# Linear attention on one core: K and V in four-head 4 KB runs as Q already was, the output moved between a group's first matmuls and its Q features, one PSUM pool

## The chip, the cores and the metric

One core of a Trainium2 chip. The metric is the device time of one execution in microseconds (us), the median of several. The "span" in a profile is the time from the first to the last instruction and is some 1.7 us shorter than the device time. All runs that are compared here were in the fast state (one run of the kernel before, beside experiments 6 and 10, was slow and stays out of the ratios); a kernel run once has the state unknown. In the profiles PE is TensorE (matmuls), DVE is VectorE, ACT is ScalarE, POOL is GpSimd and SP is SyncE. PSUM is the memory that TensorE writes its results to, and SBUF the one that the transfers fill. A "turn" is one pass of the main loop, over one group.

## The reference, cut to what matters

```python
# Q, K, V: (8, 12, 512, 64) float32
Q_feat = np.maximum(0, Q) + 1
K_feat = np.maximum(0, K) + 1
KV    = einsum('bhkd,bhkv->bhdv', K_feat, V)
K_sum = sum(K_feat, axis=2)
out   = (Q_feat @ KV) / (Q_feat @ K_sum + 1e-10)
```

There are 96 heads of 512 positions of 64 numbers. The kernel takes them in 12 groups of 8 heads. Inputs and output are 12.58 MB each, so 50.33 MB move whatever the kernel does.

## The kernel before: the parts that the change and the argument touch

Each group passes through four stages: features (DVE makes max(x+1, 1) of K and Q, ACT copies V beside a column of ones), KV (TensorE contracts K features with V, ACT copies the result "kva" out of PSUM), transposes (TensorE turns Q around, ACT copies "qt" out of PSUM), output (TensorE multiplies qt with kva, DVE takes reciprocals and multiplies, and a DMA stores).

```python
    # PSUM: qt_ps 2 tiles, kva_ps 1 tile, o_ps 2 tiles, each in its own pool
    # K, V: 8 positions (2 KB) per partition and head pair; Q: 16 positions (4 KB), four heads
    def kv_and_transpose(g):
        ...
        for h in range(2):
            for c in range(C):
                for j in range(2):           # 64 rows: one head on each half of the array
                    nc.tensor.matmul(kva_ps[:, j, h * W : h * W + W],
                        lhsT=kf[64 * j : 64 * j + 64, h, c, :, :],
                        rhs=va[64 * j : 64 * j + 64, h, c, 0:W], ...)
        ...                                   # 2 copies of kva on ACT
        for half in range(2):
            qt_ps = psum_qt.tile([P, C, P], BF16, name="qt_ps")     # a tile for each half
            for c in range(C):
                nc.tensor.transpose(qt_ps[:, c, :], qf[:, half * C + c, :, :], identity)
            nc.scalar.copy(out=qt[:, :, :, half], in_=qt_ps)
    ...
        for it in range(NG + 2):              # three groups in hand at once
            if it < NG:
                features(it)
            if 1 <= it < NG + 1:
                kv_and_transpose(it - 1)
            if it >= 2:
                output(it - 2)
            ...                               # load(it + 4), store(it - 3)
```

DVE, ACT and TensorE run these stages in the order in which the program gives them, as the timelines here show.

## Time and profile before

| | before |
|---|---|
| device time, median | 132.04 us |
| span | 129.8 us |
| bytes over the span | 388 GB/s |
| busiest compute engine (ACT) | 48% |
| ACT's wait for V from DMA | 48.6 us in 12 waits |

The lines for these are in the prediction below. Read "DMA" in the slices as the mean busy share of the 16 DMA engines in tenths, and a line of the timeline as start, length, engine, line, what was done, and in brackets how long the engine had been idle and what ended that.

### The profile page before, as it was taken

What the parts mean: (1) busy time and instruction counts of PE and PEld (TensorE: products, weight loads), DVE (VectorE), ACT (ScalarE), POOL (GpSimd) and SP (SyncE); (2) the same over time, 40 slices, a digit from 0 to 9 for tenths busy, and PEclk for the clock granted to TensorE, in tenths of its full rate; (3) what the DMA queues carried; (4) which work ended last, traced back from release to release, by engine and by line L of the source; (5) the groups of instructions that cost most, each with busy time, mean ns of one, the idle gap of its engine ahead of it and who ended that gap; (6) DMA issues with size and microseconds to landing.
All of it is one profiled execution on the core that took longest, in us unless ns stands there. A gap on an engine that the chain in (4) does not pass through costs nothing.

```text
span 129.8 us, 3048 instructions
## 1 busy us (share of the span) xinstructions
PE 59.0 (46%) x1344; PEld 50.5 (39%) x1344; DVE 57.7 (44%) x132; ACT 62.6 (48%) x73; POOL 36.1 (28%) x55
## 2 busy tenths in 40 slices
PE   0008309208758292864939119409606802933200
PEld 0007209107647191753828009308505701922100
DVE  0222212057374775727577077066227407567700
ACT  3023086590966939296690590391095096270000
POOL 6972224222332242224224222422231200202020
PEclk9999965555686959555595865875785685595555
DMA  2999999999999999999999999999999999999853
GB/s 93 321 204 195 210 194 204 210 206 211 205 209 208 209 207 206 210 207 207 277 302 207 253 331 205 231 350 191 218 347 223 212 357 418 420 417 360 341 218 121
DMA packets 19213, 32.17 MB, mean 248 GB/s; under 512 B 768, under 2 KB 12544, under 8 KB 19200
## 3 DMA queue, kind: packets, MB, share of 16 engines
q0 software_dynamic: 18672, 30.94, 106.3%
q1 hardware_dynamic: 528, 1.05, 2.1%
q8 instruction: 10, 0.16, 0.5%
q14 instruction: 3, 0.02, 0.0%
HBM read 37.75 MB, written 12.58 MB: 388 GB/s over the span
## 4 chain that ended last, share of the span: by engine, by line
DMA 72%; issue 19%; POOL 4%; POOLq 1%
DMA out_dram<-o_sb 31%; DMA k_raw<-in_K_dram 16%; DMA q_raw<-in_Q_dram 15%; DMA v_raw<-in_V_dram 9%; POOL out_dram L90 2%; POOLq L219 1%; POOL q_raw L86 1%; POOL k_raw L82 0%; POOL v_raw L85 0%; POOL identity masks.py:199 0%; POOL identity masks.py:197 0%; POOL v_aug L179 0%; POOLq L90 0%; POOLq L86 0%; POOLq L208 0%
## 5 line engine op out<-in xcount | busy, mean ns | idle before, releaser
L104 ACT COPY v_aug<-v_raw 128x1024 bf16<-128x1024 bf16 x24 | 24.1, 1056 | 48.6 <-DMA v_raw<-in_V_dram 48.6
L152 PE MATMUL o_ps<-kva,qt 64*64 64x65 bf16 x768 | 17.3, 229 | 46.9 <-DVE o_sb L165 45.8
L165 DVE TENSOR_TENSOR o_sb<-o_ps,recip 128x512 f32<-128x512 f32 x48 | 33.2, 691 | 1.6
L152 PEld LDWEIGHTS <-qt 64*64 64x64 bf16 x768 | 12.7, 137 | 52.0 <-DVE o_sb L165 48.9
L139 ACT COPY qt<-qt_ps 128x1024 bf16<-128x1024 bf16 x24 | 29.5, 1298 | 0.4
L118 PE MATMUL kva_ps<-v_aug,kf 64*128 64x129 bf16 x384 | 22.3, 302 | 15.4 <-ACT v_aug L104 10.1
L93 DVE TENSOR_SCALAR qf<-q_raw 128x2048 bf16<-128x2048 bf16 x12 | 8.3, 694 | 42.2 <-DMA q_raw<-in_Q_dram 42.2
L118 PEld LDWEIGHTS <-kf 64*128 64x128 bf16 x384 | 19.1, 137 | 16.2 <-issue 15.6
L138 PE MATMUL qt_ps<-identity,qf 128*128 128x128 bf16 x192 | 21.7, 303 | 0.1
L90 POOL DMA_DIRECT2D out_dram<-o_sb x12 | 9.3, 774 | 38.2 <-DVE o_sb L165 19.6
L138 PEld LDWEIGHTS <-qf 128*128 128x128 bf16 x192 | 18.8, 142 | 2.6 <-issue 2.2
L93 DVE TENSOR_SCALAR kf<-k_raw 128x1024 bf16<-128x1024 bf16 (+1 forms) x24 | 9.8, 450 | 11.2 <-DMA k_raw<-in_K_dram 11.1
L164 DVE RECIPROCAL recip<-o_ps 128x8 f32<-128x8 f32 x48 | 9.6, 201 | 10.5 <-PE o_ps L152 10.5
L85 POOL DMA_DIRECT2D v_raw<-in_V_dram x12 | 9.1, 759 | 17.0 <-ACT kva L127 5.4
L82 POOL DMA_DIRECT2D k_raw<-in_K_dram x11 | 8.6, 786 | 16.7 <-DVE kf L93 6.6
L86 POOL DMA_DIRECT2D q_raw<-in_Q_dram x12 | 8.4, 702 | 15.9 <-DMA k_raw<-in_K_dram 9.0
L127 ACT CAST kva<-kva_ps 64x260 bf16<-64x260 f32 x24 | 8.8, 367 | 3.5 <-PE kva_ps L118 3.4
L104 ACT ACT_TABLE_LOAD x1 | 1.3, 1283 | 0.7 <-PEq L208 0.7
masks.py:199 POOL TENSOR_SCALAR_AFFINE_SELECT identity<-identity 128x128 bf16<-128x128 bf16 x1 | 0.3, 287 | 0.1
masks.py:197 POOL MEMSET identity<- 128x128 bf16 x1 | 0.2, 244 | 0.0
L179 POOL MEMSET v_aug<- 128x16 bf16 x2 | 0.2, 175 | 0.0
L208 POOL MEMSET const-float32-0.0<- 128x1 f32 x1 | 0.1, 99 | 0.2 <-issue 0.2
(3 smaller groups left out, 0.3 us busy)
## 6 DMA issues: line engine op xcount, KB each, us to landing
out_dram<-o_sb POOLq DMA_DIRECT2D x12, 1024.0 KB, 20.0
v_raw<-in_V_dram POOLq DMA_DIRECT2D x12, 512.0 KB, 19.7
q_raw<-in_Q_dram POOLq DMA_DIRECT2D x12, 512.0 KB, 19.8
k_raw<-in_K_dram POOLq DMA_DIRECT2D x11, 512.0 KB, 19.7
k_raw<-in_K_dram SPq DMA_DIRECT2D x1, 1024.0 KB, 5.0
```

The lines of the kernel that those rows point to most:

```text
L85: nc.gpsimd.dma_start(out=v_raw, in_=v_dram[:, g * NP : g * NP + NP])
L86: nc.gpsimd.dma_start(out=q_raw, in_=q_dram[:, g * 2 : g * 2 + 2])
L90: nc.gpsimd.dma_start(out=o_dram[:, g * NP : g * NP + NP], in_=outs.pop(g))
L93: nc.vector.tensor_scalar(out=dst, in0=src, scalar1=1.0, scalar2=1.0, op0=ALU.add, op1=ALU.max)
L104: nc.scalar.copy(out=va[:, h].rearrange("p c (n x) -> p n c x", n=2)[:, :, :, 0:D], in_=v_raw[:, h:NP:2],)
L118: nc.tensor.matmul(kva_ps[:, j, h * W : h * W + W], lhsT=kf[64 * j : 64 * j + 64, h, c, :, :], rhs=va[64 * j : 64 * j + 64, h, c, 0:W], st ...
L127: nc.scalar.copy(out=kva[64 * n : 64 * n + 64, :, :, 0:D1], in_=kva_ps[64 * n : 64 * n + 64, :, 0 : 2 * W].rearrange("p j (h x) -> p j h x ...
L138: nc.tensor.transpose(qt_ps[:, c, :], qf[:, half * C + c, :, :], identity)
L139: nc.scalar.copy(out=qt[:, :, :, half], in_=qt_ps)
L152: nc.tensor.matmul(ops[n][64 * j : 64 * j + 64, c // 4, off : off + D1], lhsT=qt[64 * n : 64 * n + 64, c, 32 * b : 32 * b + 32, :], rhs=kv ...
L164: nc.vector.reciprocal(out=recip, in_=den)
L165: nc.vector.tensor_tensor(out=o_sb[:, 2 * n + h].rearrange("p (b r) d -> p b r d", b=2), in0=num, in1=recip.to_broadcast([P, 2, 4, D]), op ...
```

## The change

Its intent: larger contiguous runs for K and V, a store that follows closer behind the load, and a shorter way from the last landing to the last store. The core of the diff (cuts marked):

```diff
-    k_dram = view(K, C)
-    v_dram = view(V, C)
+    k_dram = view(K, C2)
+    v_dram = view(V, C2)
...
-    psum_qt = ... bufs=2;  psum_kva = ... bufs=1;  psum_out = ... bufs=2
+    psum = ctx.enter_context(tc.tile_pool(name="psum", bufs=4, ...))
...
+    def keys_values(g):                 # K features, V copies, KV, kva copies
...
+            for c in range(half * C, half * C + C):
+                for b in range(4):
+                    ps = slice(32 * b, 32 * b + 32)
+                    nc.tensor.matmul(kva_ps[b // 2][:, b % 2, 0:W],
+                        lhsT=kf[ps, c, :, :], rhs=va[ps, c, 0:W], ...)
...
+    def queries(g):                     # Q features, transposes, qt copies
+        qt_ps = psum.tile([P, 2, C, P], BF16, tag="ps", name="qt_ps")
         for half in range(2):
-            qt_ps = psum_qt.tile([P, C, P], BF16, name="qt_ps")
+            feature(qf[:, cs]..., q_raw[:, :, cs])
             for c in range(C):
-                nc.tensor.transpose(qt_ps[:, c, :], qf[:, half * C + c, :, :], identity)
-            nc.scalar.copy(out=qt[:, :, :, half], in_=qt_ps)
+                nc.tensor.transpose(qt_ps[:, half, c, :], qf[:, half * C + c, :, :], identity)
+            nc.scalar.copy(out=qt[:, :, :, half], in_=qt_ps[:, half])
...
+        for g in range(NG):
+            ...                         # load(g + 4), store(g - 2)
+            keys_values(g)
+            if g:
+                output(g - 1)
+            queries(g)
+        output(NG - 1)
```

The last group's store also goes out in two halves from SP instead of in one piece from GpSimd. Cut from the diff: each input stream gets 5 buffers instead of 4, and the Q features of a group become two instructions instead of one.

## The prediction

> **What bounds the kernel now.** I read the page from the top: first the span, the slices and the bytes, then the chain that ended last, then the waits, and last the timeline of two stretches.
>
> ```profile
> span 129.8 us, 3048 instructions
> ...
> DMA  2999999999999999999999999999999999999853
> ...
> HBM read 37.75 MB, written 12.58 MB: 388 GB/s over the span
> ...
> DMA 72%; issue 19%; POOL 4%; POOLq 1%
> ```
>
> All four compute engines are busy under half of the span (ACT is highest, at 48%), while the DMA engines stand at nine tenths or more from slice 2 to slice 37, and 72% of the chain that ended last is DMA. The kernel moves 37.75 + 12.58 = 50.33 MB. In the middle, one input tile of a group (1 MiB read as float32, cast to bf16 on the way) is issued about every 2.53 us, at the pace at which earlier ones land: 1.049 MB / 2.53 us = 415 GB/s. All bytes at that rate take 50.33 / 0.415 = 121.3 us. The other 8.5 us of the span are the start and the end: the slices fall to 8, 5 and 3 tenths there.
>
> The waits say the same. These two rows are engine, line, what was waited for, total us, times, longest:
>
> ```profile
> ACT v_aug L104 <- DMA v_raw<-in_V_dram: 48.6, 12, 6.9
> ...
> DVE qf L93 <- DMA q_raw<-in_Q_dram: 42.2, 12, 5.4
> ```
>
> Each group's copy of V waits for its data every time (12 of 12), by 4 us on average. The compute side has slack, and it has it because an iteration works on three groups at once: features of group i, both matmul stages of i-1, output of i-2. Within an iteration no stage needs what another stage made in that same iteration.
>
> The timeline gives the durations for the rest (start, us, engine, line, operation; xN = how many in a row):
>
> ```profile
> 24.18 2.01 ACT L104 COPY v_aug<-v_raw 128x1024 bf16<-128x1024 bf16 x2 [2.50 <-DMA v_raw<-in_V_dram]
> ...
> 26.86 2.45 ACT L139 COPY qt<-qt_ps 128x1024 bf16<-128x1024 bf16 x2
> ...
> 30.45 1.92 PE L118 MATMUL kva_ps<-v_aug,kf 64*128 64x129 bf16 x32
> 30.52 0.21 DVE L164 RECIPROCAL recip<-o_ps 128x8 f32<-128x8 f32 x1 [0.71 <-PE o_ps L152]
> ...
> 31.37 0.20 DVE L164 RECIPROCAL recip<-o_ps 128x8 f32<-128x8 f32 x1
> ...
> 32.21 0.75 DVE L93 TENSOR_SCALAR kf<-k_raw 128x1024 bf16<-128x1024 bf16 x2
> 32.30 1.89 PE L138 MATMUL qt_ps<-identity,qf 128*128 128x128 bf16 x16
> ...
> 34.12 0.63 PE L152 MATMUL o_ps<-kva,qt 64*64 64x65 bf16 x32
> ```
>
> To be seen: a V copy pair takes 2.01 us, a pair of transposed-Q copies 2.45; one output tile costs DVE 0.84 us (reciprocal at 30.52, the next at 31.37, the next work at 32.21); half of an output's matmuls 0.63. The last two lines that matter are at the end:
>
> ```profile
> 122.50 0.69 DVE L165 TENSOR_TENSOR o_sb<-o_ps,recip 128x512 f32<-128x512 f32 x1
> 123.49 0.75 POOL L90 DMA_DIRECT2D out_dram<-o_sb  x1 [4.21 <-DVE o_sb L165]
> ```
>
> After the last Q tile lands (107.47, where its feature starts) three groups' outputs are still to be made, one after the other, to 123.19; the last store then takes 6.6 us.
>
> **What the Trainium skill says.** "DMA: Bandwidth & Descriptors", section Specifications, gives a fabric ceiling of 435 GB/s; the trace's 415 GB/s is 95% of it, so longer runs have little to win. "TensorEngine Tiling (Array Packing)", section Tiling Modes, has four independent row tiles of 32x128, against two of 64x128. That two do overlap the trace shows: 32 matmuls in 1.92 us are 60 ns each, while a lone 128-column transpose takes 1.89 us / 16 = 118 ns. That four do, no run shows yet. "TensorE: Matmul & The Clock Gate", part 1, has an array clock of 1.2 GHz after an idle window and 2.4 after a busy one; the trace agrees (transposes of 118 ns are the slow state, and the granted clock in most slices is 0.5 to 0.7). "ScalarE: Activation LUTs", section What ACT_TABLE_LOAD costs, gives a copy 186 ns + 0.833 ns per element: 1.04 us for 1024, where the trace has 1.056.
>
> **The change, part by part.**
>
> (a) *4 KB runs for K and V.* The bytes stay. Q has 4 KB runs already: by what waits for them, V lands at 32.55, Q at 34.95, V at 40.05, Q at 42.54, so Q takes 2.40 and 2.49, K and V together 5.1, or 2.55 each. At best 0.1 us x 23 tiles = 2.3 us of transfer, worth something only where the DMA still sets the pace.
>
> (b) *Matmuls over 32 rows.* A partition now holds 16 positions of one of four heads, so each head contracts over 32 partitions: 768 matmuls in place of 384. If four overlap, the 64 of a group take what 32 took, 1.92 us cold, half of it (0.96) in each half. The copy of kva becomes 4 instructions of 64x130 instead of 2 of 64x260: each 0.367 - 130 x 0.00083 = 0.26 us (estimate), 1.05 us a group, 0.3 more than before.
>
> (c) *The order.* This is the large part. The instruction order of the changed program has, on ACT: V copies(g), kva copies(g), Q copies(g), V copies(g+1). On DVE: K features(g), output(g-1), Q features(g). On PE: KV(g), output(g-1), transposes(g). Follow the waits: KV(g) needs V copies(g); output(g-1) stands behind KV(g) on PE; Q features(g) stand behind output(g-1) on DVE; transposes(g) need them; Q copies(g) need the transposes; and V copies(g+1) stand behind Q copies(g) on ACT. That is a closed loop through three engines, with no overlap of one turn with the next. Its length, in us, handoffs from the trace in brackets:
>
> V copies 2.01; (0.14 to PE, as 9.98 to 10.12 in the first group) second half of KV 0.96; first half of output 0.63; four output tiles on DVE 4 x 0.84 = 3.36; first half of Q features 0.42 (0.06 to PE); eight transposes 0.94 (0.09 to ACT); Q copies 2.45. Sum 11.06 with a cold array. With some bursts warm (transposes have 1.41 for 16 in places, the output half 0.45) about 0.3 goes away: I take 10.8.
>
> Beside the loop lie: the K features of g+1, the kva copies (ACT waits for DVE then anyway), the second half of output's matmuls (its two PSUM tiles are those of kva, freed about 1.1 us after KV, before DVE has done the first two output tiles).
>
> (d) *One PSUM pool of four.* Seven tiles a turn. By the rotation only the second half of output waits for a tile of its own turn, as said: no cost.
>
> (e) *Stores and last group.* The last output waits only for its own turn, and goes out in two halves of 0.5 MB from SP. That removes two of the three outputs after the last landing, but those would cost only where the inputs set the pace.
>
> The sum. The first V lands at 8.92, and turn 0 has no output: its Q copies end near 15.7, before the second V (16.53). So turn 1 starts at 16.5; eleven turns of 10.8 end at 135.3. The last output: 0.63 + 3.36 + 0.1 = 4.1, to 139.4. The last half store: 0.4 to issue, 1.25 for 0.5 MB, about 2.4 of latency (before: 6.6 in all, less 2.5 for 1 MB, less 1.1 to issue, is 3.0) = 4, to 143.4. The time runs 1.7 above the span (131.53 against 129.8): 145.1, call it **145**.
>
> The DMA needs 7.6 + 2.5 = 10.1 us a group with its store, 7.6 without: both below 10.8, so from turn 1 on the data lies ready before its turn.
>
> **The rivals.**
> First, the DMA stays the bound, and the shorter end is the gain. For it: DMA at 9 in every slice, and about 4 us of underused transfer at the end. It would give 132 - 3 - up to 2.3 = 127 to 129. It needs a loop of 10.1 or less, with the head and tail hidden too; against it stands that copies and evacuations alone are 2.01 + 3.36 + 0.42 + 2.45 = 8.24 with no matmul counted.
> Second, the loop with a warm array: KV half 0.5, output 0.45, transposes 0.47, sum 9.95; 16.5 + 109.5 + 8.0 + 1.7 = 136. For it: the granted clock is not always low; against it: PE has the same work in a longer span with idle stretches of over 2 us each turn.
> Third, four row tiles do not overlap better than two: each half of KV takes 1.92, and the second ends 1.15 + 1.92 + 1.92 = 4.99 after the V copies began instead of 3.11, which adds 1.9 a turn, 21 in all: 166. For it: untested here; against it: pairs overlap nearly perfectly.
>
> **Range and chances.** The loop makes it slower in all but the first rival. Between the warm loop (136) and a partly failing overlap I take 138 to 153. To be faster or the same, the serial loop must be wrong, and I find no way round it in the order: 0.04 faster by over 2%, 0.06 within, 0.90 slower.
>
> **What would show it.** Right: ACT's wait for V data falls from 48.6 us to a few, and a wait of some 4 us a turn before the Q copies, on the transposes, takes its place; the chain runs through ACT, PE and DVE in turn; V copies start about every 10.8 us; DMA slices drop below 9; The third rival: the second KV half of 32 takes near 1.9 us. The second: transposes near 60 ns each. Wrong: V copies that still wait for the V transfer in the middle of the span.

## The result, and the profile after

The changed kernel takes 159.32 us (159.03 to 159.56, 4 runs), against 132.04. The ratio is 1.2155, with a 95% interval of 1.2002 to 1.2309. (The measuring program takes a ratio from the fast runs; it is not quite the ratio of the medians.) Executions over 1.5% slower than the fastest of the same kernel are left out of the means. It is slower, as forecast, but well beyond the range.

The page of the changed kernel, the lines that answer to those shown of before:

```profile
span 157.5 us, 3854 instructions
...
DMA  5999999999999999999999999999700700700615
GB/s 154 267 210 212 211 210 212 212 214 209 210 211 212 227 324 204 302 252 212 338 219 274 278 210 339 215 262 409 293 4 1 270 0 4 266 0 4 266 53 214
...
HBM read 37.75 MB, written 12.58 MB: 320 GB/s over the span
...
PE 33%; DVE 28%; ACT 18%; issue 10%; DMA 7%; POOL 2%; POOLq 0%
DVE o_sb L170 21%; PE qt_ps L142 14%; PE kva_ps L117 14%; ACT qt L143 10%; ACT v_aug L110 7%; DMA v_raw<-in_V_dram 7%; PE o_ps L157 5%; DVE recip L169 4%; DVE qf L98 3%; POOL q_raw L85 0%; POOL k_raw L81 0%; POOL v_raw L84 0%; POOL identity masks.py:199 0%; POOL identity masks.py:197 0%; POOL v_aug L184 0%
```

The chain that ended last was 72% DMA and is now 7% DMA; PE, DVE and ACT in turn make up 79%. The DMA slices still stand at 9 as far as slice 27: loads run ahead of their use while buffers are free, so a full DMA row alone does not say that DMA is the bound. After slice 28 (counted from 0) it has almost nothing to move but one store in every third slice, which is one a turn.

The waits of the changed kernel (engine, line, what was waited for, total us, times, longest):

```profile
ACT qt L143 <- PE qt_ps L142: 63.6, 23, 4.9
...
PE qt_ps L142 <- ACT qt L143: 15.2, 11, 1.4
...
ACT v_aug L110 <- DMA v_raw<-in_V_dram: 6.0, 1, 6.0
```

ACT waits for V once, for the first tile. In its place stand waits of engines for each other. The timeline shows one whole turn:

```profile
64.47 2.00 ACT L110 COPY v_aug<-v_raw 128x1024 bf16<-128x1024 bf16 x2
...
65.58 2.00 PE L117 MATMUL kva_ps<-v_aug,kf 32*128 32x129 bf16 x64 [2.30 <-ACT v_aug L110]
...
67.51 0.66 PE L157 MATMUL o_ps<-kva,qt 64*64 64x65 bf16 x32
...
68.20 0.21 DVE L169 RECIPROCAL recip<-o_ps 128x8 f32<-128x8 f32 x1 [7.00 <-PE o_ps L157]
...
71.57 0.75 DVE L98 TENSOR_SCALAR qf<-q_raw 128x1024 bf16<-128x1024 bf16 x2
...
72.05 1.03 PE L142 MATMUL qt_ps<-identity,qf 128*128 128x128 bf16 x8 [2.87 <-DVE qf L98]
...
73.11 1.29 ACT L143 COPY qt<-qt_ps 128x1024 bf16<-128x1024 bf16 x1 [4.64 <-PE qt_ps L142]
74.46 1.01 PE L142 MATMUL qt_ps<-identity,qf 128*128 128x128 bf16 x8 [1.38 <-ACT qt L143]
...
75.51 1.29 ACT L143 COPY qt<-qt_ps 128x1024 bf16<-128x1024 bf16 x1 [1.10 <-PE qt_ps L142]
76.66 2.01 ACT L110 COPY v_aug<-v_raw 128x1024 bf16<-128x1024 bf16 x2
```

Each line starts where the one above lets it. (The first matmuls, at 65.58, need only the first of the two V copies; the second copy runs beside the first half of KV.) From V copies to V copies is 76.66 - 64.47 = 12.19 us, and it is 12.19 or 12.20 in six of the ten turns between two V copies that have an output (11.98 to 12.41 in the others). The line that the prediction did not have is the one at 74.46: the second eight transposes start only after ACT has copied the first eight, although they go to another bank. Both halves are one PSUM tile now, and the built program makes TensorE wait for ACT's read of a tile before writing into that tile again.

Against the prediction's own sum:

| step of a turn | predicted, us | measured, us |
|---|---|---|
| V copies, handoff, second half of KV | 3.11 | 67.51 - 64.47 = 3.04 |
| first half of the output's matmuls | 0.63 | 68.20 - 67.51 = 0.69 |
| four output tiles on DVE | 3.36 | 71.57 - 68.20 = 3.37 |
| first Q features, handoff | 0.48 | 72.05 - 71.57 = 0.48 |
| eight transposes, handoff | 1.03 | 73.11 - 72.05 = 1.06 |
| from the first Q copy to the next V copies | 2.45 | 76.66 - 73.11 = 3.55 |
| sum | 11.06 (10.8 used) | 12.19 |

In the first row the profile's chain goes through one V copy and then all of KV, 1.11 + 1.93; the prediction went through both V copies and then half of KV. The two ways differ by 0.07 us.

### The profile page after: what moved, and what is told of

Its sections match the earlier page's. It is cut to its first block, busy times and chain, and to the rows that moved or that the text cites. A ratio compares the mean times of both kernels' runs of the same rounds, so it can differ in the third digit from the quotient of the medians.

```text
span 157.5 us, 3854 instructions
## 1 busy us (share of the span) xinstructions
PE 63.8 (40%) x1728; PEld 53.4 (34%) x1728; DVE 58.4 (37%) x144; ACT 65.3 (41%) x97; POOL 34.5 (22%) x54
## 4 chain that ended last, share of the span: by engine, by line
PE 33%; DVE 28%; ACT 18%; issue 10%; DMA 7%; POOL 2%; POOLq 0%
DVE o_sb L170 21%; PE qt_ps L142 14%; PE kva_ps L117 14%; ACT qt L143 10%; ACT v_aug L110 7%; DMA v_raw<-in_V_dram 7%; PE o_ps L157 5%; DVE recip L169 4%; DVE qf L98 3%; POOL q_raw L85 0%; POOL k_raw L81 0%; POOL v_raw L84 0%; POOL identity masks.py:199 0%; POOL identity masks.py:197 0%; POOL v_aug L184 0%
## 5 line engine op out<-in xcount | busy, mean ns | idle before, releaser
L143 ACT COPY qt<-qt_ps 128x1024 bf16<-128x1024 bf16 x24 | 31.0, 1292 | 63.7 <-PE qt_ps L142 63.6
L142 PE MATMUL qt_ps<-identity,qf 128*128 128x128 bf16 x192 | 23.5, 299 | 48.6 <-DVE qf L98 32.0
L117 PE MATMUL kva_ps<-v_aug,kf 32*128 32x129 bf16 x768 | 23.9, 306 | 34.8 <-ACT v_aug L110 34.8
L142 PEld LDWEIGHTS <-qf 128*128 128x128 bf16 x192 | 18.5, 137 | 52.2 <-DVE qf L98 33.7
L117 PEld LDWEIGHTS <-kf 32*128 32x128 bf16 x768 | 20.7, 136 | 37.5 <-issue 36.6
L92 POOL DMA_DIRECT2D out_dram<-o_sb x11 | 8.6, 785 | 61.1 <-DVE o_sb L170 51.5
L157 PEld LDWEIGHTS <-qt 64*64 64x64 bf16 x768 | 14.1, 150 | 7.5 <-issue 5.4
L128 ACT CAST kva<-kva_ps 64x130 bf16<-64x130 f32 x48 | 10.3, 264 | 13.8 <-PE kva_ps L117 13.7
L98 DVE TENSOR_SCALAR kf<-k_raw 128x1024 bf16<-128x1024 bf16 (+1 forms) x24 | 10.7, 486 | 7.3 <-DMA k_raw<-in_K_dram 7.3
L81 POOL DMA_DIRECT2D k_raw<-in_K_dram x11 | 7.9, 715 | 17.0 <-DMA v_raw<-in_V_dram 4.8
L98 DVE TENSOR_SCALAR qf<-q_raw 128x1024 bf16<-128x1024 bf16 x24 | 9.6, 444 | 3.6 <-DMA q_raw<-in_Q_dram 3.6
```

Of the source, the lines that this page charges most:

```text
L92: nc.gpsimd.dma_start(out=o_to, in_=o_sb)
L98: nc.vector.tensor_scalar(out=dst, in0=src, scalar1=1.0, scalar2=1.0, op0=ALU.add, op1=ALU.max)
L117: nc.tensor.matmul(kva_ps[b // 2][:, b % 2, 0:W], lhsT=kf[ps, c, :, :], rhs=va[ps, c, 0:W], start=(c == 0), stop=(c == C2 - 1),)
L128: nc.scalar.copy(out=kva[ps, h, :, 0:D1], in_=kva_ps[h][ps, :, D * n : D * n + D1])
L142: nc.tensor.transpose(qt_ps[:, half, c, :], qf[:, half * C + c, :, :], identity)
L143: nc.scalar.copy(out=qt[:, :, :, half], in_=qt_ps[:, half])
```

## The experiments

Theory A is that this loop of a turn sets the time, with the shared tile on it. The rivals are that the layout (32-row matmuls, 4 KB runs), ACT's load as such, the distance of the output from its matmuls, or the DMA set it. The kernels ran beside runs of the kernel before (median 131.4 us). The changed kernel itself ran in a call of its own, in which the kernel before took 132.04, so differences against 159.32 carry some 0.6 us of that. Every result was correct.

**1. A PSUM tile for each half of the transposed Q.**

```diff
-        qt_ps = psum.tile([P, 2, C, P], BF16, tag="ps", name="qt_ps")
         for half in range(2):
+            qt_ps = psum.tile([P, 2, C, P], BF16, tag="ps", name="qt_ps")
```

> The changed kernel with one edit: each half of the transposed Q gets a PSUM tile of its own instead of half of one shared tile. Theory A (the serial loop of a turn is the bound, and the shared tile put the second eight transposes and a handoff, 1.14 us, on it): a turn falls from 12.19 to about 11.05 us, the wait of the transposes on the Q copies (15.2 us in 11 waits) is gone, and the time falls by 12 x 1.14 = 13.7, from 159.3 to about 145.6. Rival B (the loop is not the bound; DMA with fewer outstanding transfers or the row tiles are): 157 to 160.

Measured: 145.73 us, ratio to before 1.1074 (1.1006 to 1.1142). The fall of 159.32 - 145.73 = 13.6 us is close to the 13.7 expected, partly by luck: turn 0 gains nothing, because turn 1 has to wait for the second V anyway (it starts at 15.68, against 15.48), and each later turn falls by some 1.25 us rather than 1.14. The timeline of this run has the sixteen transposes in one piece, both Q copies back to back, and the next V copies at once:

```profile
67.27 1.54 PE L142 MATMUL qt_ps<-identity,qf 128*128 128x128 bf16 x16 [2.87 <-DVE qf L98]
...
68.00 2.45 ACT L143 COPY qt<-qt_ps 128x1024 bf16<-128x1024 bf16 x2 [4.29 <-PE qt_ps L142]
...
70.30 2.01 ACT L110 COPY v_aug<-v_raw 128x1024 bf16<-128x1024 bf16 x2
```

Turns take 10.6 to 11.2 us, and the transposes' wait on the Q copies is gone from the waits. From the first Q copy to the next V copies it is now 70.30 - 68.00 = 2.30 us, where the shared tile had 3.55. The shared tile was worth 13.6 us. With it away the kernel is where the prediction had put it (145), though there two small misses cancel: turn 1 starts 0.8 us earlier than predicted, and turns of mostly 10.94 instead of 10.8 add 1.5.

**2. Queries before the output.**

```diff
             keys_values(g)
+            queries(g)
             if g:
                 output(g - 1)
-            queries(g)
```

> The changed kernel with two calls swapped: the Q features and transposes of a group come before the output of the group before it. Theory A (the loop closes only because the Q features stand behind the output on DVE): the loop is broken, DVE's 3.36 us and the output matmuls leave it, a turn needs about 7.7 us on ACT, less than the DMA's 10, so the DMA is the bound again and the time is 126 to 130, below the kernel before. Rival B (32-row matmuls, the one PSUM pool or the store order slow it): 140 or more.

Measured: 132.83 us, ratio 1.0087 (1.0018 to 1.0156), so within 2% of the kernel before. One swap takes back 26.5 of the 27.3 us, which none of the rivals allows. But it missed 126 to 130. In its timeline the turn is 9.74 us over long stretches, and what KV waits for is new:

```profile
36.05 0.75 DVE L98 TENSOR_SCALAR kf<-k_raw 128x1024 bf16<-128x1024 bf16 x2
...
45.79 0.75 DVE L98 TENSOR_SCALAR kf<-k_raw 128x1024 bf16<-128x1024 bf16 x2
46.26 1.65 PEld L117 LDWEIGHTS <-kf 32*128 32x128 bf16 x64 [2.57 <-DVE kf L98]
46.27 1.92 PE L117 MATMUL kva_ps<-v_aug,kf 32*128 32x129 bf16 x64 [2.43 <-DVE kf L98]
```

The data of that group had landed before; its K features stand behind the last output on DVE, and so a second, shorter loop closed: K features, KV, transposes with the wait on the shared tile, output, DVE, K features. I had checked only the loop that I meant to break.

**3. The second Q copy made twice.** A cost is doubled at a place that lies on the loop.

```diff
             nc.scalar.copy(out=qt[:, :, :, half], in_=qt_ps[:, half])
+            if half:
+                nc.scalar.copy(out=qt[:, :, :, half], in_=qt_ps[:, half])
```

> The changed kernel with the second Q copy of each group made twice (same result). Theory A: the Q copies lie on the loop, so each turn grows by one copy, 1.15 to 1.3 us, twelve times: 173 to 175. Rival B (ACT is 41% busy and has room): within 1 us of 159.3.

Measured, one run: 175.04 us, 15.7 more. The turn grows from 12.19 to 13.51, so by 1.32, and 12 x 1.32 = 15.8. The V copies now start after the added one:

```profile
57.09 2.00 ACT L110 COPY v_aug<-v_raw 128x1024 bf16<-128x1024 bf16 x2
...
69.44 1.29 ACT L145 COPY qt<-qt_ps 128x1024 bf16<-128x1024 bf16 x1
70.60 2.00 ACT L110 COPY v_aug<-v_raw 128x1024 bf16<-128x1024 bf16 x2
```

**4. All kva copies made twice.** About as much more work on the same engine, at another place.

```diff
                 nc.scalar.copy(out=kva[ps, h, :, 0:D1], in_=kva_ps[h][ps, :, ...])
+            for h in range(2):
+                nc.scalar.copy(out=kva[ps, h, :, 0:D1], in_=kva_ps[h][ps, :, ...])
```

> The changed kernel with all four kva copies of each group made twice (same result): 0.87 us more work a turn on the same engine, but at a place where ACT then waits for the transposes for 4.6 us. Theory A: off the loop, so 159 to 160.5. Rival C (any work on ACT counts, the engine is the bound): plus 12 x 0.87 = 10 us, about 170.

Measured, one run: 159.98 us. The turn is 12.19 as before. It does delay something: the second half of the output's matmuls starts 0.86 us after the first half ended, instead of 0.20, because it needs the PSUM tiles of kva. These matmuls end at 70.20, and the third output tile's turn on DVE comes at 70.24, in the same step of 0.84 us as the tiles before it. So the delay still fits, but only just:

```profile
69.38 0.82 PE L161 MATMUL o_ps<-kva,qt 64*64 64x65 bf16 x32 [0.86 <-ACT kva L132]
...
70.24 0.20 DVE L173 RECIPROCAL recip<-o_ps 128x8 f32<-128x8 f32 x1
```

So 0.87 us more per turn on ACT left the turn at 12.19 at one place, and 1.3 us cost all of itself at another. ACT's share (41%) says neither; the place in the loop does. The slack at the first place is nearly used up by this: more work there would be expected to reach the loop, which no run here tried.

**5. K and V back in 2 KB runs, with 64-row matmuls, in the changed kernel.**

```diff
-    k_dram = view(K, C2)
-    v_dram = view(V, C2)
+    k_dram = view(K, C)
+    v_dram = view(V, C)
...
-                for b in range(4):
-                    ps = slice(32 * b, 32 * b + 32)
+                for j in range(2):
+                    ps = slice(64 * j, 64 * j + 64)
...                                       # the tile shapes and the PSUM tile of each half follow
```

> The changed kernel, with K and V back in 2 KB runs and 64-row matmuls and nothing else undone. Theory A: neither is on the loop (KV takes the same 1.9 us either way), so the turn stays 12.2 and the time is 159 to 161, one microsecond more for the later first V. Rival E (the 32-row matmuls or the four heads to a tile cost the time): back towards 132.

Measured, one run: 160.32 us, turns of mostly 12.2. The layout is not on the loop; the first V comes 1.1 us later (9.10 against 7.99), as expected. From the start of KV to the start of the next matmuls it is 1.93 us in either form: 65.58 to 67.51 in the turn of the changed kernel shown above, 66.72 to 68.65 here. The third rival of the prediction is out.

```profile
66.72 2.00 PE L117 MATMUL kva_ps<-v_aug,kf 64*128 64x129 bf16 x32 [2.30 <-ACT v_aug L110]
...
68.65 1.51 PE L157 MATMUL o_ps<-kva,qt 64*64 64x65 bf16 x64
```

**6. The output two groups behind, at the same place.**

```diff
-LAG = 2
+LAG = 3
...
-            if g:
-                output(g - 1)
+            if g >= 2:
+                output(g - 2)
             queries(g)
+        output(NG - 2)
         output(NG - 1)
```

> The changed kernel with the output two groups behind, as before the change, but at the same place in the turn (after the first matmuls, before the Q features), and stores three behind. Theory A (the loop closes through the order on the in-order engines, not through the data of the group): a turn with output still takes 12.2 us; one turn more has no output at the start (4 us less) and one output more stands at the end (4 us more): 158 to 161. Rival F (the shorter distance between a group's matmuls and its output is what costs): 130 to 136.

Measured, one run: 158.84 us. The added turn without output takes 8.44 us, all later ones 12.2 to 12.3. The lag in groups does not matter here. What closes the loop is where the output stands in the queues of PE and DVE.

**7. Both edits: queries first, and two tiles.** The diffs of experiments 1 and 2 together.

> The changed kernel with both edits: queries before the output, and a PSUM tile for each half of the transposed Q. With the queries first alone a second loop was left (K features of the next group stand behind the output on DVE): K features 0.39, KV 1.92, transposes with their wait for the Q copy 3.4, output half 0.64, four output tiles 3.4 = 9.74 us a turn, as measured, beside the DMA's 10. Theory A: the second tile takes about 1.3 us off that loop (turn 8.4), the DMA is the bound from the middle on, the last Q lands near 104 instead of 113, and the time is 125 to 128. Rival D (the DMA already was the bound in the middle, the loop only ran beside it): 131.5 to 133.

Measured: 128.55 us, ratio 0.9775 (0.9733 to 0.9817), faster than the kernel before, though not clearly by 2%. With the shared tile away the second loop is shorter than the DMA's time for a group once stores flow (turns of 7.4 to 8.5 us early, of 9.4 to 10.7 later), and V copies wait for their data again:

```profile
84.77 2.01 ACT L110 COPY v_aug<-v_raw 128x1024 bf16<-128x1024 bf16 x2 [4.09 <-DMA v_raw<-in_V_dram]
...
94.88 2.01 ACT L110 COPY v_aug<-v_raw 128x1024 bf16<-128x1024 bf16 x2 [3.54 <-DMA v_raw<-in_V_dram]
```

Rival D is out. But the time lies 0.55 us above the expected range: the last Q landed at 107.51 instead of near 104, which is when it landed in the kernel before (107.47). So, in these two traces, the gain over the kernel before shows after the last landing: 19.2 us are left from there to the end of the span, instead of 22.3.

**8. The same with 2 KB runs and 64-row matmuls.** The diffs of experiments 5 and 7 together.

> The same as the run with both edits, but K and V in the old 2 KB runs with 64-row matmuls. If the DMA is the bound there, 4 KB runs are worth (2.53 - 2.47) us x 36 tiles = 2.2 us at most: this is 1.5 to 3 us slower than the run with both edits. If runs of 4 KB are worth nothing: the same within 0.5 us.

Measured: 129.84 us, ratio 0.9871 (0.9835 to 0.9908). The intervals of the two ratios do not touch, so 4 KB runs, with the matmul form that goes with them, are worth 129.84 - 128.55 = 1.3 us where DMA is the bound. That is somewhat less than I expected. Where it is not the bound they change no turn (experiment 5). What makes up the other 1.6 us to the kernel before (131.41) was not taken apart: the order, the fifth input buffer, the earlier store and the split last store all differ.

**9. Both edits, and in the last turn the output of group 10 ahead of the last queries.**

```diff
-            queries(g)
+            if g < NG - 1:
+                queries(g)
             if g:
                 output(g - 1)
+        queries(NG - 1)
         output(NG - 1)
```

> The run with both edits, but in the last turn alone the output of group 10 comes before the queries of group 11, so that it need not wait for the last Q. Saves up to 3.4 us of DVE work after the last landing; if the stores still in the queue set the end (five of 2.5 us), the time is the same within 0.5 us, else 1 to 3 us less.

Measured: 127.91 us, ratio 0.9727 (0.9688 to 0.9766). That is 0.6 us under experiment 7, between the two outcomes that the expectation named. The intervals of the two ratios overlap, but both contain the noise of the kernel before. The six runs of each differ in the mean by 0.61 us (95% interval 0.22 to 1.00), so a small gain is likely. Against before it is a gain of 2.7%. Its page:

```profile
DMA  4999999999999999999999999999999999999992
GB/s 78 336 211 209 213 212 211 211 213 211 215 207 216 206 211 214 209 304 285 215 266 320 210 240 348 208 218 363 216 210 341 248 211 315 417 422 412 414 378 83
...
DMA 55%; PE 15%; DVE 14%; issue 5%; ACT 5%; POOL 1%; ACTq 1%; POOLq 0%
```

Here the row of nines reaches to the last slice but one, the stores run at 412 to 422 GB/s in slices 34 to 37 (counted from 0), and the chain is mostly DMA again.

**10. The same, with the K features of the next group ahead of the output.** This breaks the second loop as well.

```diff
             if g < NG - 1:
                 queries(g)
+                keys(g + 1)          # K features, taken out of keys_values (cut here)
             if g:
                 output(g - 1)
```

> The run with both edits and the last turn mended, with the K features of the next group moved ahead of the output, which breaks the second loop too. If the DMA is the bound there, as its slices of 9 show, nothing is gained: 127.5 to 128.5, the same as without within 0.6 us. If the second loop still costs something in the early turns without stores: 126 to 127.3.

Measured: 127.70 us, ratio 0.9730 (0.9691 to 0.9769): the same as experiment 9, by the ratios. It was run at another time. The turns that took 7.8 to 8.1 us in experiment 9, before stores flow, take 7.5 here, and the end does not move: with DMA as the bound, a loop that is shorter than DMA's pace over the whole costs nothing.

## Why the prediction was wrong

*Direction and mechanism: right.* The closed loop through ACT, PE and DVE is in the timeline step by step, at the predicted lengths within 0.07 us for the first five steps. ACT's wait for V fell from 48.6 to 6.0 us, and waits of 4.6 us before the first Q copies took its place. Experiments 2 and 6 show that the order closes the loop.

*The step that failed: part (d), "No cost" for the one pool.* I followed the rotation of the four buffers and asked which tile waits for which buffer. I did not ask what happens inside a tile. The diff moves the making of the tile out of the loop over halves, so two halves that each had a tile now share one. The second eight transposes then wait for the first copy, and they came onto the loop (1.05 us with their handoff to ACT, and 0.05 for the handoff to them): 3.55 us where part (c) has 2.45, so 1.10 more than predicted. The waits show it: "PE qt_ps L142 <- ACT qt L143: 15.2, 11, 1.4". Experiment 1 takes this away and gets 13.6 us back. There the same step takes 2.30, so the shared tile costs 1.25 a turn; part (c) had 0.15 too much for two copies in a row, since in the timeline the next ACT instruction starts 0.15 before the recorded end of the one before (68.00 + 2.45 against 70.30).

*A second, smaller step: the deduction in part (c), from 11.06 to 10.8, for warm bursts.* In the changed kernel the transposes ran at the slow pace in nearly every turn, so the unreduced sum was the right one: 11 x 0.26 = 2.9 us.

*The account in span.* Predicted 143.4. Turn 1 began at 15.48 instead of 16.5: minus 1.0, for the first tiles landed earlier (the first V at 7.99 instead of 8.92). Eleven turns longer by 12.19 - 10.8 = 1.39: plus 15.3, of which 12.1 are the 1.10 of the shared tile (13.75 for the tile, less 1.65 for the copies counted too long) and 2.9 the deduction. From the last Q copy to the end 7.96 instead of 8.1. The sum is 157.5, as measured.

*The rivals.* The warm loop (136) did not come. Row tiles that fail to overlap (166) are refuted by experiment 5. The DMA bound with a shorter end (127 to 129) is wrong for the changed kernel, but it is just what the order of experiments 7, 9 and 10 reaches, at 127.7 to 128.6. *The signs named:* "DMA slices drop below 9" came only after slice 27, since loads run ahead; as a sign of the bound it was a poor one.

*My use of the DMA ceiling.* I set 415 GB/s, which counts float32 bytes read, against a ceiling of the SBUF side. But the cast halves these bytes before they are written: the page before the change has 32.17 MB in its packets against 50.33 MB moved at the HBM, and its GB/s row reads some 210 in the slices before stores flow, and 417 to 420 in slices 33 to 35, after the last load. So "95%" compared two different things, and whether longer runs have little to win was not settled by it. Experiment 8 measured it: 1.3 us.

```profile
GB/s 93 321 204 195 210 194 204 210 206 211 205 209 208 209 207 206 210 207 207 277 302 207 253 331 205 231 350 191 218 347 223 212 357 418 420 417 360 341 218 121
DMA packets 19213, 32.17 MB, mean 248 GB/s; under 512 B 768, under 2 KB 12544, under 8 KB 19200
```

*My use of the clock.* I took granted clocks of 0.5 to 0.7 as agreeing with the slow pace of the matmuls. The runs do not bear this out as a rule: the last section has the numbers.

## What to carry to other kernels

When a change reorders stages on engines that keep their order, write down for each engine what stands behind what, follow the waits round until they close or end, and add up each loop that closes; compare the longest with the time that the bound resource needs for a turn, and look for the next loop when you break one. Then look at every tile that is now made outside a loop and was made inside it: a wait goes with the tile, not with the part of it that is used. To tell whether work lies on such a loop, double it: here the same engine took 0.87 us more a turn without a longer turn at one place, and paid 15.7 us in all for one more copy a turn at another. A doubling that costs nothing shows that its place has that much slack, not that it has more.

## What the Trainium skill lacked or had wrong

- "TensorE: Matmul & The Clock Gate", part 1, ties the pace of matmuls to the gate's state, and warns that its trace events have been seen to be unreliable. The warning holds here, and should stand ahead of the rule. Four runs of the changed kernel had mean granted clocks of 0.572, 0.924, 0.807 and 0.587, and took 159.26, 159.38, 159.56 and 159.03 us. Within experiment 2 the transposes of a ten-us window (us, PE busy and count, ACT busy and count, granted clock, DMA share, GB/s) took the same time at both readings, 1.00 and 0.50:

```profile
30.00:40.00 10.00, 2.04 (x16) 2.86 (x3) 1.00 1.13 212
...
90.00:100.00 10.00, 2.04 (x16) 2.85 (x3) 0.50 1.10 262
```

- "TensorEngine Tiling (Array Packing)" gives only a theoretical factor for four row tiles (part 3 of the clock page has 3.07 over one tile at 512 columns). Here 64 matmuls of 32 rows and 129 columns took 1.92 us, as 32 of 64 rows did: 30 ns against 60 ns each, so a full factor of two over two tiles.
- "DMA: Bandwidth & Descriptors" has measured bandwidth by size of transfer for HBM to SBUF; on short runs it gives a fixed cost per packet, but no measured step from 2 KB to 4 KB runs. Here 4 KB runs against 2 KB runs for K and V, with a cast, were worth 1.3 us of 129.8, or 1.0% (experiments 7 and 8).
- No page that I read says that the built program's waits go by tile. "PSUM — Partial Sum Buffer" treats collisions by bank and quadrant; the two halves of the transposed Q lie in different banks, and the wait between them still cost 1.25 us a turn until each had a tile of its own (experiment 1).
